# Two MLPs: the norm's factor moved behind the down product, and three small table products moved into the first MLP

## The chip, the cores and the metric

The kernel runs on one core of a Trainium2 chip. The core has a matrix engine (TensorE, PE in the profile, with PEld for its weight loads), a vector engine (VectorE, DVE), an activation engine (ScalarE, ACT), a general engine (GpSimd, POOL), and DMA queues, of which the one of SyncE (SP) carries nearly all loads. The metric is the device time of one execution in microseconds (us), as the median over several runs.

## The reference, cut to what matters

The input is 256 tokens of width 1024 in float32. Two transformer layers follow, each an attention block and then an MLP, and after them a third, different block. Only the MLP, its norm and one bias table matter here:

```python
def rms_norm(x, g):
    y = xf * lax.rsqrt(jnp.mean(xf * xf, axis=-1, keepdims=True) + EPS)
    return y * g

def sq_relu_mlp(h, w_up, w_down):            # D_FF = 4096
    return jnp.square(jax.nn.relu(h @ w_up)) @ w_down

for layer in range(2):
    h = h + attention(...)                   # a different one in each layer
    h = h + sq_relu_mlp(rms_norm(h, mlp_norm[layer]), mlp_w_up[layer], mlp_w_down[layer])
```

The third block has three attention groups of 8 heads each, whose logits get a relative position bias `rel_bias_2[bucket(distance), head]`.

Write r for the factor rsqrt(mean + EPS) of a token. It is positive, so relu(r z) = r relu(z), and the square of that is r*r times relu(z) squared. The factor can therefore be left out ahead of the up product and applied as r*r to the token's row of the down product.

## The kernel before, in words

The residual `hres` stays on the chip as two tiles of 128 tokens, t = 0 and 1, each 128x1024. Every product is made of three single ones: each float32 operand is split into a rounded high part and a remainder (`whi`/`wlo` for weights, `..h`/`..l` for activations), and high x high, high x low and low x high are added up in PSUM. A weight part of 1 MB is loaded by SyncE's queue into one of 3 buffers `raw`, split by ScalarE (L252, high) and VectorE (L255, low) into one of 4 buffers, and used by TensorE.

An MLP, `mlp(i)`, runs like this. The norm (`norm_x`) makes for each t the factor: two squares with a running sum on ScalarE (L175), an add and a scale on VectorE (L177, L156), and the power -1/2 on GpSimd (L158). Then VectorE multiplies the row by factor and gain in two halves (L193), TensorE transposes the 8 blocks (L165) into the two PSUM banks `tr`, and ScalarE and VectorE split the result into `mxh` and `mxl` (L169). The hidden width is done in 8 chunks of 512. Chunk 0 (`up_tok`) is computed token by token, so it can begin with t = 0 alone; chunk 1 and later (`up`, L310 to L313) by feature, with all 256 tokens at once. From chunk 2 on, `step(c - 2)` adds an older chunk to the down product (L361 to L364), which stays in four PSUM banks to the end. `last([6, 7])` finishes the down product, t = 0 first, and adds each half row to the residual (`add_res`, L318).

After the last chunk the first MLP calls `biases_2`, which for three groups loads a 33x512 one-hot table (tile `oh`, L428, from two buffers), multiplies it by 8 columns of the bias table (tile `bt`, L430, in a bank of `tr`), copies the result on ScalarE (`bts`, L432) and stores it from ScalarE's queue to a table `vec_b` in DRAM (L433). The third block reads the tables much later. Then `layer_b` begins: it loads small constants (L441), takes transposes of the unnormed residual (L165) and their split (`bxh`, `bxl`), and multiplies with two narrow matrices, the first with 288 columns (L275 to L278).

The program's order is not the order of each engine. A planner simulates the program, gives each instruction a place in its engine's queue, and prefers, of what is ready, what comes first in the program. Tiles of one name share a few buffers in the order in which the program asks for them. Loads marked `keep_in_program_order` (L441) and instructions inside `behind` are held back on purpose. On the chip each queue then runs strictly in that order.

Of the kernel before, what the change touches and what calls it, by code (L numbers as in the profile page):

```python
# [14 lines left out]
OP = mybir.AluOpType  # L15
# [74 lines left out]
def block_kernel(ctx: ExitStack, tc: tile.TileContext, a, out: bass.AP):  # L90
    nc = tc.nc
    V, A, G, PE = nc.vector, nc.scalar, nc.gpsimd, nc.tensor
# [9 lines left out]
    def nm(s):  # L102
        uid[0] += 1
        return f"{s}_{uid[0]}"

    def t4(s, dt=F32, cols=1024):
        return sp.tile([P, cols], dt, tag="x4", name=nm(s), bufs=N4)

    def t2(s, dt=F32, cols=512):
        return sp.tile([P, cols], dt, tag="x2", name=nm(s), bufs=N2)  # L110

    def tj(s, cols=512):
        return sp.tile([P, cols], F32, tag="sq", name=nm(s), bufs=NSQ)

    def tpt(s):
        return sp.tile([P, 512], F32, tag="pT", name=nm(s), bufs=NPT)

    SMALL = dict(bn=(24, 2), ss=(1, 4), ss2=(2, 4), lr=(1, 2), gk=(64, 1), gkq=(64, 1), gq=(64, 1), kj=(64, 2), kr=(32, 2), krj=(32, 2), kro=(32, 2),
                 l=(16, 6), nx=(16, 6), scq=(4, 8), rr=(16, 8), rv=(16, 4), ce=(8, 6), pre=(16, 2), ssr=(1, 2))

    def sm(s, cols=8):
        w, n = SMALL.get(s, (8, 2))
        return sp.tile([P, w], F32, tag="s_" + s, name=nm(s), bufs=n)
# [7 lines left out]
    def pop(s):  # L131
        return pp.tile([P, 512], F32, tag="po", name=nm(s), bufs=NPO)

    def lgp(s):
        return pp.tile([P, 512], F32, tag="lg", name=nm(s), bufs=NLG)

    def bcast_row(dst, src_1d, n):
        G.dma_start(dst, row(src_1d, n))
# [6 lines left out]
    hres = [cp.tile([P, D], F32, name=f"h{t}") for t in range(2)]  # L145
# [7 lines left out]
    def rsqrt_eps(ss, scale, n, eps=EPS):  # L153

        v = sm("rv", n)
        V.tensor_scalar(v[:, :n], ss, scale, eps, op0=OP.mult, op1=OP.add)  # L156
        r = sm("rr", n)
        G.tensor_tensor(r[:, :n], v[:, :n], mhalf[:, :n], op=OP.pow)  # L158
        return r[:, :n]

    def transposes(src, n, ps=None, w=P):

        ps = trp("tr") if ps is None else ps
        for i in range(n):
            PE.transpose(ps[:w, i * P:(i + 1) * P], src[:, i * w:(i + 1) * w], ident)  # L165
        return ps
# [4 lines left out]
    def rms_stats(h):  # L171
        ss2 = sm("ss2", 2)
        for i in range(2):
            j = tj("sq")
            A.activation(j, h[:, i * 512:(i + 1) * 512], AF.Square, accum_out=ss2[:, i:i + 1])  # L175
        ss = sm("ss", 1)
        V.tensor_tensor(ss[:, :1], ss2[:, 0:1], ss2[:, 1:2], op=OP.add)  # L177
        return rsqrt_eps(ss[:, :1], 1.0 / D, 1)

    def norm_T(h, r, gain, x, t):  # L180

        if r is not None or gain is not None:
            hns = t4("hn")
        for i in range(2):
            c = slice(i * 512, (i + 1) * 512)
            hn = h[:, c] if r is None and gain is None else hns[:, c]
            if gain is None:
                if r is not None:
                    V.tensor_scalar(hn, h[:, c], r, None, op0=OP.mult)
            elif r is None:  # L190
                V.tensor_tensor(hn, h[:, c], gain[:, c], op=OP.mult)
            else:
                V.scalar_tensor_tensor(hn, h[:, c], r, gain[:, c], op0=OP.mult, op1=OP.mult)  # L193
            ps = transposes(hn, 4)
            put(x, i, t, ps.rearrange("p (k n) -> p k n", k=4))

    mark = []
# [9 lines left out]
    def norm_x(x, gain, fold=True):  # L207


        holds, rs = [tuple(mark[1:])], []  # L210
        for t in range(2):
            if fold:
                rs.append(rms_stats(hres[t]))
                norm_T(hres[t], None, gain, x, t)
            else:
                norm_T(hres[t], rms_stats(hres[t]), gain, x, t)
            holds.append(tuple(mark))
        return holds, rs
# [12 lines left out]
    def put(x, i, t, src):  # L231

        mark[:] = split(x[0][i][:, :, t * P:(t + 1) * P], x[1][i][:, :, t * P:(t + 1) * P], src)

    def xs(x, k, t):
        return x[k // 4][:, k % 4, t * P:(t + 1) * P]
# [28 lines left out]
    def wparts(w, KT, c0, n, k0=0, gain=None, by_k=False):  # L265
        return [(g, min(4, KT - g), wsplit(w, k0 + g, min(4, KT - g), c0, n, gain, by_k and g == 0))
                for g in range(0, KT, 4)]
# [47 lines left out]
    def add_res(t, ci, ps, scale=None):  # L315
        h = hres[t][:, ci * 512:(ci + 1) * 512]
        if scale is None:
            V.tensor_tensor(h, ps, h, op=OP.add)  # L318
        else:
            V.scalar_tensor_tensor(h, ps, scale, h, op0=OP.mult, op1=OP.add)  # L320

    def gain_row(src, n=D, s="gain"):
        g = t4(s) if n > 512 else t2(s)
        bcast_row(g[:, :n], src, n)
        return g
# [17 lines left out]
    def down_acc(w, us, nc_):  # L343

        banks = {}

        def bank(ci, t):
            if (ci, t) not in banks:
                banks[ci, t] = pop("dn") if (ci, t) == (1, 1) else lgp("dn")
            return banks[ci, t]  # L350

        def load(c, ci):
            return wparts(w, len_u(us[c]), ci * 512, 512, k0=4 * c)[0]

        def run(c, ci, t, part):
            ps, u = bank(ci, t), us[c]
            kt = len_u(u)
            _, _, (wh, wl) = part
            for k in range(kt):
                s0 = xs(u[0], k, t)  # L360
                PE.matmul(ps, s0, wh[:, k, :], start=(c == 0 and k == 0), stop=False)  # L361
                PE.matmul(ps, s0, wl[:, k, :], start=False, stop=False)  # L362
            for k in range(kt):
                PE.matmul(ps, xs(u[1], k, t), wh[:, k, :], start=False, stop=(c == nc_ - 1 and k == kt - 1))  # L364

        def step(c):
            for ci in range(2):
                part = load(c, ci)
                for t in range(2):
                    run(c, ci, t, part)  # L370

        def last(cs):
            parts = [[load(c, ci) for c in cs] for ci in range(2)]
            for t in range(2):
                for ci in range(2):
                    for c, part in zip(cs, parts[ci]):
                        run(c, ci, t, part)
                    add_res(t, ci, banks[ci, t])
        return step, last

    def mlp(i):
        g = gain_row(a["mlp_norm"][i])
        x = xpair("mx")
        holds, _ = norm_x(x, g, fold=False)
        us = []
        w = a["mlp_w_up"][i]

        def square(ps):
            r = t2("r")
            A.activation(r, ps, AF.Relu)  # L390
            sq = t2("sq")
            A.activation(sq, r, AF.Square)
            return sq

        def up_tok(c):
            u = xpair("u", 4)

            def evac(t, ps):
                tp = transposes(square(ps), 4).rearrange("p (k n) -> p k n", k=4)
                put(u, 0, t, tp)  # L400
            dense_by_tile([(x, 8, w, c * 512, 512, None, evac)], holds=holds[:1])
            us.append(u)

        def up(c):
            u = xpair("u", 4)
            with behind(holds[1] if c == 1 else None):
                parts = wparts(w, 8, c * 512, 512)
            for pr in range(2):
                put_feat(u, pr, square(feat_bank("up", x, parts, pr)))
            us.append(u)  # L410

        step, last = down_acc(a["mlp_w_down"][i], us, 8)
        up_tok(0)
        up(1)
        for c in range(2, 8):
            step(c - 2)
            up(c)
        last([6, 7])
        if i == 0:
            biases_2()  # L420

    def len_u(u):
        return u[0][0].shape[1]

    def bias_rows(which, K, M, c0, vec):

        oh = tpt("oh")
        nc.sync.dma_start(oh[:33, :], a["c_oh"][:, which, :])  # L428
        ps = trp("bt")
        PE.matmul(ps[:M, :], rb[:K, c0:c0 + M], oh[:K, :], start=True, stop=True)  # L430
        sb = tj("bts")
        A.activation(sb[:M, :], ps[:M, :], AF.Copy)  # L432
        nc.scalar.dma_start(vec, sb[:M, :])  # L433

    vec_a = dr.tile([16, 512], F32, name="vec_a")
    vec_b = [dr.tile([8, 512], F32, name=f"vec_b{g}") for g in range(3)]
# [6 lines left out]
    def load_consts():  # L443
# [6 lines left out]
            gcols[nm_] = cp.tile([P, 8], F32, name="gc" + nm_)  # L450
            ldk(gcols[nm_], src.rearrange("(k p) -> p k", p=P))
        return chmask

    def biases_2():
        for g in range(3):
            bias_rows(1 + g, 33, 8, 16 + 8 * g, vec_b[g])

    def quad(tl, Sk):
        return tl[:, :4 * Sk].rearrange("p (h s) -> p h s", h=4)
# [816 lines left out]

    layer_a()
    mlp(0)
    layer_b()
    mlp(1)  # L1280
    block2()
    ffn()
# [27 lines left out]
```

## Time and profile before

| | |
|---|---|
| Runs of the kernel | 1163.79, 1168.25 and 1168.85 us, median 1168.25 |
| The profiled execution's own time | 1167.43 us |
| Its span, first to last instruction | 1165.6 us |
| Mean granted clock of TensorE | 0.99 of full speed |

The span lies 1.83 us under the time of the same execution. In the profile, a row of the timeline shows the start in us from the span's start, the time that it covers, the engine, the line, the operation, the tile written and the tiles read, and how many instructions were merged into it; in brackets stands the idle time of the engine just before, and what ended it. [...]

### The profile page before, as it was taken

The page shows a single profiled execution, that of the slowest core. Times are in us where ns is not written, and L with a number is a line of the kernel's source. Part 1 is how long each engine was busy: PE and PEld are TensorE (multiplying, and loading weights), DVE is VectorE, ACT ScalarE, POOL GpSimd, SP SyncE. Part 2 cuts the span into 40 slices and gives each one's busy share as a digit, 9 for nine tenths or more (in the row PEclk, how much of TensorE's full clock was granted, in tenths as well). Part 3 has the DMA queues.
Part 4 walks back from the last instruction along what each step waited for, and adds up shares of the span by engine and source line. Part 5 has one row for each costly group of instructions (what it writes and reads, how often), then busy time and mean ns, then how long its engine had stood idle before and what let it go on. Part 6 is the DMA issues. An engine that isn't in the chain of part 4 may idle for free.

```text
span 1165.6 us, 17291 instructions
## 1 busy us (share of the span) xinstructions
PE 1130.8 (97%) x6912; PEld 998.9 (86%) x6912; DVE 676.4 (58%) x1190; ACT 613.0 (53%) x1070; POOL 95.9 (8%) x120
## 2 busy tenths in 40 slices
PE   7989999999989999999999999999999999999997
PEld 7767798998778888998989999889888878999996
DVE  6884655445569565445446885665474556544545
ACT  7654554455568455455446564464564435443443
POOL 1310000000048200000000000010000030000000
PEclk9999999999999899999999999999999999999999
DMA  9720646556345126656536644554544434546541
GB/s 287 260 91 5 204 158 216 183 179 179 93 145 178 55 73 217 202 177 202 196 100 236 217 145 145 190 190 137 177 157 145 171 136 162 196 167 216 199 134 65
DMA packets 105383, 191.92 MB, mean 165 GB/s; under 512 B 6616, under 2 KB 22960, under 8 KB 105304
## 3 DMA queue, kind: packets, MB, share of 16 engines
q1 hardware_dynamic: 104072, 187.17, 48.3%
q0 software_dynamic: 1040, 3.54, 1.0%
q8 instruction: 54, 0.88, 0.3%
q14 instruction: 25, 0.20, 0.1%
q10 hardware_dynamic: 192, 0.12, 0.0%
HBM read 189.68 MB, written 1.13 MB: 164 GB/s over the span
## 4 chain that ended last, share of the span: by engine, by line
PE 67%; DVE 1%; issue 1%; POOL 1%; ACT 1%; POOLq 0%; DVEq 0%
PE acc L275 7%; PE acc L276 7%; PE acc L278 7%; PE dn L361 4%; PE dn L362 4%; PE dn L364 4%; PE tr L165 3%; PE up L310 2%; PE up L313 2%; PE up L311 2%; PE po L500 2%; PE qk L311 2%; PE qk L310 2%; PE qk L313 2%; PE fg L311 1%; PE fp L311 1%
## 5 line engine op out<-in xcount | busy, mean ns | idle before, releaser
L255 DVE TENSOR_TENSOR wlo<-raw,whi 128x1024 fp32r<-128x1024 f32 (+3 forms) x340 | 387.0, 1179 | 209.9 <-ACT whi L252 209.2
L252 ACT ACTIVATE whi<-raw 128x1024 fp32r<-128x1024 f32 (+3 forms) x340 | 323.2, 1008 | 209.8 <-PE dn L364 82.8
L310 PE MATMUL up<-mxh,whi 128*128 128x256 f32 x448 | 110.9, 281 | 0.0
L311 PE MATMUL up<-mxl,whi 128*128 128x256 f32 x448 | 110.7, 280 | 0.0
L362 PE MATMUL dn<-wlo,uh 128*128 128x512 f32 x256 | 100.5, 393 | 0.0
L361 PE MATMUL dn<-whi,uh 128*128 128x512 f32 x256 | 100.4, 394 | 0.0
L158 POOL TENSOR_TENSOR rr<-rv,mhalf 128x1 f32<-128x1 f32 (+2 forms) x42 | 42.6, 1017 | 652.5 <-DVE rv L156 630.8
L310 PEld LDWEIGHTS up<-mxh,whi 128*128 128x128 f32 x448 | 84.4, 188 | 0.7
L311 PEld LDWEIGHTS up<-mxl,whi 128*128 128x128 f32 x448 | 84.2, 188 | 0.7
L275 PE MATMUL acc<-whi,cxh 128*128 128x512 f32 (+1 forms) x192 | 74.5, 389 | 0.0
L276 PE MATMUL acc<-wlo,cxh 128*128 128x512 f32 (+1 forms) x192 | 72.4, 378 | 0.0
L313 PE MATMUL up<-mxh,wlo 128*128 128x256 f32 x448 | 70.8, 280 | 0.0
L364 PE MATMUL dn<-whi,ul 128*128 128x512 f32 x256 | 69.6, 394 | 0.0
L313 PEld LDWEIGHTS up<-mxh,wlo 128*128 128x128 f32 x448 | 60.3, 188 | 0.0
L364 PEld LDWEIGHTS dn<-whi,ul 128*128 128x128 f32 x256 | 48.0, 188 | 11.2
L361 PEld LDWEIGHTS dn<-whi,uh 128*128 128x128 f32 x256 | 48.1, 188 | 10.6
L362 PEld LDWEIGHTS dn<-wlo,uh 128*128 128x128 f32 x256 | 48.1, 188 | 10.6
L278 PE MATMUL acc<-whi,cxl 128*128 128x512 f32 (+1 forms) x192 | 50.6, 382 | 0.0
L310 PE MATMUL qk<-cxh,whi 128*128 128x256 f32 x192 | 49.1, 288 | 0.0
L169 DVE TENSOR_TENSOR ul<-sq,uh 128x512 fp32r<-128x512 f32 x28 | 19.4, 692 | 50.6 <-ACT uh L169 50.3
L311 PE MATMUL qk<-cxl,whi 128*128 128x256 f32 x192 | 48.2, 282 | 0.0
L484 ACT ACTIVATE lg<-lg,nx 128x128 f32<-128x128 f32 (+1 forms) x80 | 35.4, 446 | 14.8 <-DVE nx L544 14.6
(413 smaller groups left out, 2443.5 us busy)
## 6 DMA issues: line engine op xcount, KB each, us to landing
raw<-in_w_in SPq DMA_DIRECT2D x38, 1024.0 KB, 5.0
raw<-in_mlp_w_up SPq DMA_DIRECT2D x32, 1024.0 KB
raw<-in_mlp_w_down SPq DMA_DIRECT2D x32, 1024.0 KB, 5.0
raw<-in_w_gate SPq DMA_DIRECT2D x10, 1024.0 KB, 5.2
raw<-in_w_up SPq DMA_DIRECT2D x10, 1024.0 KB, 5.2
raw<-in_w_down SPq DMA_DIRECT2D x10, 1024.0 KB, 4.9
raw<-in_w_in SPq DMA_DIRECT2D x6, 688.0 KB
raw<-in_a_w_in SPq DMA_DIRECT2D x4, 1024.0 KB
```

The costliest lines, as they stand in the source:

```text
L158: G.tensor_tensor(r[:, :n], v[:, :n], mhalf[:, :n], op=OP.pow)
L252: A.activation(hi[:, c], raw[:, c], AF.Copy)
L255: V.tensor_tensor(lo[:, c], raw[:, c], hi[:, c].bitcast(F32), op=OP.subtract)
L275: PE.matmul(o, s0, wh[:, k, :], start=(g + k == 0), stop=False)
L276: PE.matmul(o, s0, wl[:, k, :], start=False, stop=False)
L278: PE.matmul(o, xs(xl, g + k, t), wh[:, k, :], start=False, stop=(g + k == KT - 1))
L310: PE.matmul(o, s0, xh[(g + k) // 4][:, (g + k) % 4, :], start=(g + k == 0), stop=False)
L311: PE.matmul(o, s0, xl[(g + k) // 4][:, (g + k) % 4, :], start=False, stop=False)
L313: PE.matmul(o, wl[:, k, col:col + P], xh[(g + k) // 4][:, (g + k) % 4, :], start=False, stop=(g + k == KT - 1))
L361: PE.matmul(ps, s0, wh[:, k, :], start=(c == 0 and k == 0), stop=False)
L362: PE.matmul(ps, s0, wl[:, k, :], start=False, stop=False)
L364: PE.matmul(ps, xs(u[1], k, t), wh[:, k, :], start=False, stop=(c == nc_ - 1 and k == kt - 1))
```

## The change

The MLP's norm is left without its factor: gain, transposes and split work on the raw residual. The factors are made by a new function `factors`, called after chunk 1: the same statistics, then the factor times itself. `last` passes the two results to `add_res`, which multiplies the PSUM row by it while adding (L320 instead of L318). Both MLPs are changed so. `biases_2` is removed, and its three calls of `bias_rows` are made in the first MLP behind chunks 3, 4 and 5.

```diff
-    SMALL = dict(bn=(24, 2), ss=(1, 4), ...
+    SMALL = dict(r2=(1, 2), bn=(24, 2), ss=(1, 4), ...
...
-        def last(cs):
+        def last(cs, scale=None):
...
-                    add_res(t, ci, banks[ci, t])
+                    add_res(t, ci, banks[ci, t], scale and scale[t])
...
     def mlp(i):
         g = gain_row(a["mlp_norm"][i])
         x = xpair("mx")
-        holds, _ = norm_x(x, g, fold=False)
+        holds = [tuple(mark[1:])]
+        for t in range(2):
+            norm_T(hres[t], None, g, x, t)
+            holds.append(tuple(mark))
+        r2 = []
+
+        def factors():
+            for t in range(2):
+                r = rms_stats(hres[t])
+                q = sm("r2", 1)
+                V.tensor_tensor(q[:, :1], r, r, op=OP.mult)
+                r2.append(q[:, 0:1])
...
         up_tok(0)
         up(1)
+        factors()
         for c in range(2, 8):
             step(c - 2)
             up(c)
-        last([6, 7])
-        if i == 0:
-            biases_2()
+            if i == 0 and 3 <= c <= 5:
+                bias_rows(c - 2, 33, 8, 8 * c - 8, vec_b[c - 3])
+        last([6, 7], r2)
...
-    def biases_2():
-        for g in range(3):
-            bias_rows(1 + g, 33, 8, 16 + 8 * g, vec_b[g])
```

## Rows read from the trace of the kernel before

**Rows 1.** The page's busy times and shares of the span.
```profile
PE 1130.8 (97%) x6912; PEld 998.9 (86%) x6912; DVE 676.4 (58%) x1190; ACT 613.0 (53%) x1070; POOL 95.9 (8%) x120
```

**Rows 2.** A window inside the first MLP (PE, PEld, DVE, ACT, POOL, clock, DMA).
```profile
200.00:285.00 85.00, 85.00 (x557) 77.42 (x556) 39.36 (x37) 43.19 (x52) 1.14 (x2) 1.00 0.55 183
```

**Rows 3.** Timeline of TensorE, start of the first MLP.
```profile
125.91 1.09 PE L278 MATMUL acc<-whi,mxl 128*128 128x512 f32 x4
129.21 1.75 PE L165 MATMUL tr<-ident,hn 128*128 128x128 f32 x8 [2.21 <-DVE hn L193]
...
133.67 0.28 PE L310 MATMUL up<-mxh,whi 128*128 128x256 f32 x1
```

**Rows 4.** Timeline of VectorE, the same stretch.
```profile
120.38 1.28 DVE L318 TENSOR_TENSOR h<-acc,h 128x512 f32<-128x512 f32 x2
...
128.31 1.42 DVE L193 SCALAR_TENSOR_TENSOR hn<-h,rr,gain 128x512 f32<-128x512 f32 x2 [0.45 <-POOL rr L158]
```

**Rows 5.** Windows around idle stretches of TensorE (columns as in rows 2).
```profile
129.20:133.00 3.80, 3.79 (x14) 2.99 (x15) 1.91 (x3) 1.19 (x2) 0.00 (x0) 0.55 0.86 285
...
310.20:314.00 3.80, 3.80 (x18) 3.37 (x18) 2.86 (x16) 3.35 (x8) 0.00 (x0) 0.55 0.12 25
...
306.20:308.20 2.00, 1.93 (x5) 0.27 (x4) 0.69 (x1) 0.59 (x1) 0.00 (x0) 1.00 0.03 9
...
321.30:322.90 1.60, 0.00 (x0) 0.00 (x0) 0.70 (x3) 0.67 (x2) 0.87 (x2) 1.00 0.07 27
322.90:326.00 3.10, 3.06 (x23) 3.06 (x24) 1.53 (x4) 1.37 (x3) 0.00 (x0) 1.00 0.01 3
```

**Rows 6.** Timeline of TensorE, end of the first MLP, start of layer_b.
```profile
305.23 1.09 PE L364 MATMUL dn<-whi,ul 128*128 128x512 f32 x4
306.25 1.88 PE L430 MATMUL bt<-oh,rb 33*8 33x512 f32 x4
309.32 1.02 PE L430 MATMUL bt<-oh,rb 33*8 33x512 f32 x2 [1.19 <-DMA oh<-in_c_oh]
310.26 1.86 PE L165 MATMUL tr<-ident,h 128*128 128x128 f32 x8
311.89 0.61 PE L275 MATMUL acc<-whi,bxh 128*128 128x288 f32 x1
...
313.96 0.60 PE L165 MATMUL tr<-ident,h 128*128 128x128 f32 x4
```

**Rows 7.** Timeline of SyncE's queue, the same stretch.
```profile
307.30 0.32 SPq L428 DMA_DIRECT2D oh<-in_c_oh  x1
307.67 0.38 SPq L441 DMA_DIRECT2D rp<-in_c_rope  x1
```

**Rows 8.** Timeline of TensorE, start of the second MLP.
```profile
436.67 1.04 PE L165 MATMUL tr<-ident,hn 128*128 128x128 f32 x8
438.01 0.50 PE L275 MATMUL acc<-whi,mxh 128*128 128x512 f32 x1 [0.30 <-ACT mxh L169]
```

**Rows 9.** Single lines: instructions, and ns as minimum, median and maximum.
```profile
L320 DVE SCALAR_TENSOR_TENSOR h<-acc,h x4: 681/688/692, 957.6 to 970.4; 128x512 f32<-128x512 f32 x4
...
L193 DVE SCALAR_TENSOR_TENSOR hn<-h,rr,gain x16: 744/746/752, 102.5 to 973.8; 128x512 f32<-128x512 f32 x16
...
L175 ACT ACTIVATE sq<-h x28: 613/630/637, 3.5 to 1159.8; 128x512 f32<-128x512 f32 x28
```

**Rows 10.** Timelines of ScalarE, VectorE and TensorE in mid MLP.
```profile
211.11 0.60 ACT L390 ACTIVATE r<-up 128x512 f32<-128x512 f32 x1 [3.63 <-PE up L313]
...
214.89 3.90 ACT L252 ACTIVATE whi<-raw 128x1024 fp32r<-128x1024 f32 x4 [1.85 <-PE up L311]
...
215.99 4.63 DVE L255 TENSOR_TENSOR wlo<-raw,whi 128x1024 fp32r<-128x1024 f32 x4 [2.22 <-ACT whi L252]
...
216.56 0.39 PE L361 MATMUL dn<-whi,uh 128*128 128x512 f32 x1
...
227.75 0.28 PE L310 MATMUL up<-mxh,whi 128*128 128x256 f32 x1
```

More of the change, by code (lines that the diff above doesn't have):

```diff
@@ L116, in tpt @@
         return sp.tile([P, 512], F32, tag="pT", name=nm(s), bufs=NPT)
-    SMALL = dict(bn=(24, 2), ss=(1, 4), ss2=(2, 4), lr=(1, 2), gk=(64, 1), gkq=(64, 1), gq=(64, 1), kj=(64, 2), kr=(32, 2), krj=(32, 2), kro=(32, 2),
+    SMALL = dict(r2=(1, 2), bn=(24, 2), ss=(1, 4), ss2=(2, 4), lr=(1, 2), gk=(64, 1), gkq=(64, 1), gq=(64, 1), kj=(64, 2), kr=(32, 2), krj=(32, 2), kro=(32, 2),
                  l=(16, 6), nx=(16, 6), scq=(4, 8), rr=(16, 8), rv=(16, 4), ce=(8, 6), pre=(16, 2), ssr=(1, 2))
```

## The prediction

> **What bounds the kernel now.** I read the page first: TensorE is busy for 97% of the span [rows 1], so I take the time to be TensorE's queue plus its gaps, and any other engine's work to cost nothing while TensorE is fed. The windows inside the MLPs bear this out: 85.00 us busy out of 85.00, at full clock, with VectorE and ScalarE at half load [rows 2]. A change here can pay only where TensorE stands still, and in what its clock does after a standstill. So I listed the waits of TensorE's queue and went to the timelines of the three places that the diff touches.
>
> At the start of the first MLP the last four products of token tile 0 begin at 125.91, and then TensorE waits 2.21 us for VectorE's `hn`, the normed row of tile 1 [rows 3]. On VectorE the residual was complete at 121.66 (120.38 + 1.28), but `hn` began only at 128.31, behind GpSimd's factor [rows 4]: 6.7 us went by for the statistics. [...]
>
> At the end of the first MLP the last down products begin at 305.23. Then come two bias products, a wait of 1.19 us for the third one-hot table, the third product, and only then the transposes for layer_b; the first product of layer_b begins at 311.89 [rows 6]. The queue of SyncE shows why the table was late: two buffers hold the first two, so the third load was issued at 307.30, after the first product [rows 7]. Again the clock is 0.55, from 310.2 to 314.0 [rows 5]. The second MLP starts better: its second transposes wait for nothing, and 0.30 us is lost before the next product [rows 8].
>
> **The norm, first MLP.** Removed ahead of the transposes are the statistics of both tiles; the multiplication by factor and gain becomes one by gain. It costs 0.746 us per half row now [rows 9], and with one operand fewer I take it as no dearer. With the residual whole at 121.66 the two halves can be ready near 123.2 (121.66 + 2 x 0.75), more than two microseconds before the last products of tile 0 begin, so the transposes can go between them without a wait. What would stay of the stretch: products of 512 columns come every 0.233 us (48 of them between 216.56 and 227.75 [rows 10]), so tile 0's stream ends at 125.91 + 4 x 0.233 = 126.84. Until 133.67 TensorE did 8 transposes and 8 such products. At full clock these are at most 1.04 [rows 8] and 8 x 0.233 = 1.87, together 2.9, where 6.83 passed. Gain 3.9 us. The lower bound is that `hn` keeps its place in VectorE's queue and only its 0.45 us of waiting for GpSimd goes [rows 4]: 0.5. I take 3.9, since the residual is there so long before.
>
> **The norm, second MLP.** The 0.30 us before 438.01 goes the same way [rows 8]: 0.3, between 0 and 0.6.
>
> **The factors.** They come back as four squares on ScalarE, 0.63 us each [rows 9], 2.5 us per MLP, and a few operations on single columns. They stand behind chunk 1, and nothing reads them until the last additions, behind the last chunk. What hides them is the reserve of the weight splits: the four casts that begin at 214.89 and VectorE's halves of them are done by 220.62 (215.99 + 4.63), and TensorE goes on to the next chunk only at 227.75 [rows 10], so about 7 us of lead remain. Cost 0, or 2.5 if that lead were gone.
>
> **The scaled addition.** The trace has no `add_res` in the MLP with a column of factors. The nearest is L320, which does the same with a constant: 0.688 us for the half row out of PSUM; with a column and two SBUF operands it is 0.746 [rows 9]. So 0 to 0.06 us each, of which one per MLP is exposed: 0. [...]
>
> **The bias products, where they were.** From 306.16 (305.23 + 4 x 0.233) to 313.96 TensorE did the six bias instructions, 8 transposes and 8 products of 288 columns [rows 6]. Without the bias the transposes of tile 0 come first: its residual has long been added. In the second MLP it is 1.34 us from the start of such transposes to the first product [rows 8]. The 8 products took 2.07 at mostly half clock, so some 1.04 at full. That is 2.4 instead of 7.8: gain 5.4. What could be late next is the split `bxl` on VectorE, were it queued behind operations on the constants, whose loads stood behind the third table in SyncE's queue [rows 7]; that queue is now free of it, so I expect them earlier. If they bind all the same, I put the gain at half, 2.7.
>
> **The bias products, where they go.** Six instructions at 0.43 us (four take 0.86 longer than two, 1.88 against 1.02 [rows 6]) are 2.6 us in a stretch without gaps: paid in full. ScalarE gets the three copies and their three DMA issues, under the same 7 us of lead; behind them stand casts, for which TensorE would wait last. SyncE gets the third load earlier, behind the first product; the other two were already loaded long ahead.
>
> **Sum.** 3.9 + 0.3 + 5.4 - 2.6 = 7.0 us of 1167.43, the profiled execution's own time (span 1165.6 and 1.83 around it): 1160.4. The median of the runs is 0.8 higher, from which it would be 1161.2; I give 1160.8.
>
> **The rivals.** A: the next wait takes the place of the bias gap in layer_b, and the move gains 2.7 - 2.6 = nothing: gain 4.2, or 1163.6. For it: layer_b waits for short chains elsewhere, such as 1.6 us idle at 321.3 [rows 5]. Against: tile 0's residual is ready, and nothing else stands in its way that I see.
>
> B: the planner keeps tile 1's `hn` behind the splits of chunk 1, so the change doesn't do there what it says. The first term falls from 3.9 to 0.5: 1164.2. For it: VectorE stood idle for only 0.45 us ahead of `hn` [rows 4], so it had other work between. Against: the planner prefers what comes first in the program, and `hn` does.
>
> C: the clock falls at the light bias products in mid MLP. A fall as at 129.2 costs 0.45 x 3.8 = 1.7 us [rows 5]; three cost 5.1: 1165.9. For it: at 310.2 the clock was down although the idle wait before was only 1.2 us, after products of 33 rows and 8 columns; an idle 1.6 us at 321.3 left it at 1.00 [rows 5]. Against: 1.9 us of those very products ran at 1.00 [rows 5], and each pair now lasts 0.86 us between dense work. [...]
>
> D, slower: a bias copy stands in ScalarE's queue ahead of the casts, and waits there for a product that TensorE has placed behind a half chunk of 11.2 us (216.56 to 227.75 [rows 10]). It decides from a wait of 7 us on. At three places this is 3 x (11.2 - 7) = 12.6, and a fall of the clock each, 5.1: 1178.5. For it: both queues are strict. Against: ScalarE's wait for TensorE there is 3.63 us [rows 10], and the planner would have to be wrong by a multiple of that.
>
> **How the numbers follow.** Forecast 0.60, A 0.15, B 0.12, C 0.06, D 0.07. One half per cent, 5.8 us, is about what a measurement of this kernel can tell from no change; the bound is 1162.4. The forecast lies under it, D above 1174.1, the others between: faster 0.60, same 0.33, slower 0.07. The range begins at 1157.0: the sum from the profiled execution (1160.4) with 0.3 more in the second MLP, the 1.6 us wait of layer_b gone, since ScalarE is freer there, and one fall of the clock fewer (1.7). It ends at 1167.0, where A and B meet (2.8 and 3.4 above the forecast); C lies inside.
>
> **What would show it.** After the change TensorE has no wait for `hn` at the first MLP's start and a clock of 1.00 there; transposes of `h` follow directly on the last L364 at the end, and the first product of layer_b comes 1.3 us later; the span from the first MLP's start to there is shorter by 3.9 - 2.6 up to the last L364, and by 5.4 more after it. Six L430 instructions stand in mid MLP, at 0.43 us, with PEclk 1.00. The additions are L320 at about 0.7 us. I am wrong if windows in mid MLP are no longer full, or if what was gained is lost again in layer_b's attention, whose clock I have left as it was.

## The result, and the profile after

The kernel after takes 1160.54 us as the median of 5 runs (1155.89 to 1161.48), the kernel before 1168.25 beside it (5 runs, 1163.79 to 1169.15). The ratio is 0.9934 with a 95% interval of 0.9917 to 0.9951: faster by 7.7 us. That is more than the half per cent (5.8 us) that the prediction set, though the near end of the interval, 5.7 us, does not clear it. Forecast were 1160.8 us, and a chance of 0.60 for faster by that much. The profiled execution after took 1161.48 us with a span of 1159.7; the one before took 1167.43.

The page shows TensorE as busy as before [rows 1]:

```profile
PE 1128.4 (97%) x6912; PEld 996.8 (86%) x6912; DVE 675.7 (58%) x1194; ACT 612.0 (53%) x1070; POOL 95.1 (8%) x120
```

The timeline of TensorE after, from the first norm of the first MLP to the second MLP:

```profile
103.71 0.66 PE L165 MATMUL tr<-ident,o 128*128 128x128 f32 x4 [1.27 <-DVE o L695]
...
128.11 1.10 PE L278 MATMUL acc<-whi,mxl 128*128 128x512 f32 x4
129.05 1.03 PE L165 MATMUL tr<-ident,hn 128*128 128x128 f32 x8
130.39 0.50 PE L275 MATMUL acc<-whi,mxh 128*128 128x512 f32 x1 [0.30 <-ACT mxh L169]
...
132.35 0.28 PE L310 MATMUL up<-mxh,whi 128*128 128x256 f32 x1
...
192.93 1.02 PE L443 MATMUL bt<-oh,rb 33*8 33x512 f32 x2
193.88 0.50 PE L361 MATMUL dn<-whi,uh 128*128 128x512 f32 x1
...
307.36 1.10 PE L364 MATMUL dn<-whi,ul 128*128 128x512 f32 x4
308.29 1.04 PE L165 MATMUL tr<-ident,h 128*128 128x128 f32 x8
309.58 0.40 PE L275 MATMUL acc<-whi,bxh 128*128 128x288 f32 x1 [0.25 <-ACT bxh L169]
...
310.74 0.60 PE L165 MATMUL tr<-ident,h 128*128 128x128 f32 x4
...
318.58 0.44 PE L165 MATMUL tr<-ident,lc 128*128 128x128 f32 x2 [0.50 <-DVE lc L768]
...
356.99 0.64 PE L165 MATMUL tr<-ident,k 128*96 128x128 f32 x4 [1.74 <-POOL k L831]
...
381.29 0.77 PE L165 MATMUL tr<-ident,p 128*128 128x128 f32 x2 [1.66 <-ACT p L493]
...
412.59 0.38 PE L165 MATMUL tr<-ident,oB 128*128 128x128 f32 x2
...
424.67 0.60 PE L165 MATMUL tr<-ident,hn 128*128 128x128 f32 x4
425.02 0.48 PE L275 MATMUL acc<-whi,mxh 128*128 128x512 f32 x1
...
432.02 0.50 PE L275 MATMUL acc<-whi,mxh 128*128 128x512 f32 x1 [0.30 <-ACT mxh L169]
...
433.99 0.28 PE L310 MATMUL up<-mxh,whi 128*128 128x256 f32 x1
```

Four rows of the kernel before, for the places that the rows ahead of the prediction do not show:

```profile
101.52 0.66 PE L165 MATMUL tr<-ident,o 128*128 128x128 f32 x4 [0.79 <-DVE o L686]
...
322.94 0.44 PE L165 MATMUL tr<-ident,lc 128*128 128x128 f32 x2 [1.65 <-DVE lc L759]
...
418.07 0.38 PE L165 MATMUL tr<-ident,oB 128*128 128x128 f32 x2
...
439.98 0.28 PE L310 MATMUL up<-mxh,whi 128*128 128x256 f32 x1
```

Read against [rows 3], the wait of 2.21 us for tile 1's `hn` is gone: the transposes follow tile 0's last products at 129.05. From those products to the first L310 it is now 4.24 us (128.11 to 132.35), where it was 7.76. Read against [rows 6], the transposes of `h` follow the last L364, and from that L364 to the second transposes it is 3.38 us (307.36 to 310.74), where it was 8.73. One wait is longer: at 103.71 TensorE waits 1.27 us for `o`, and it was 0.79 before (101.52).

VectorE's timeline shows why, for better and for worse:

```profile
102.36 0.69 DVE L191 TENSOR_TENSOR hn<-h,gain 128x512 f32<-128x512 f32 x1
102.97 0.68 DVE L695 TENSOR_TENSOR o<-po,rl 128x512 f32<-128x512 f32 x1
...
122.58 1.28 DVE L318 TENSOR_TENSOR h<-acc,h 128x512 f32<-128x512 f32 x2
...
124.44 1.28 DVE L191 TENSOR_TENSOR hn<-h,gain 128x512 f32<-128x512 f32 x2
```

The residual of tile 1 is whole at 123.86, and `hn` begins at 124.44 without waiting for a factor. For tile 0 the same readiness puts an `hn` ahead of the attention's `o`, for which TensorE stands still.

Windows of the kernel after (columns as in rows 2, the clock being that granted to TensorE as a share of full speed): the start of the first MLP, mid MLP with two of the bias places, the start of layer_b, and two stretches of layer_b's attention.

```profile
129.00:132.80 3.80, 3.50 (x22) 2.85 (x21) 2.84 (x7) 2.09 (x4) 0.56 (x1) 1.00 1.00 316
...
200.00:285.00 85.00, 85.00 (x547) 75.69 (x546) 37.63 (x35) 41.62 (x52) 0.00 (x0) 1.00 0.53 177
...
307.30:311.00 3.70, 3.45 (x24) 2.94 (x24) 2.01 (x5) 2.07 (x5) 0.40 (x1) 1.00 0.35 121
...
340.00:370.00 30.00, 25.97 (x147) 22.41 (x146) 25.20 (x60) 23.92 (x59) 26.40 (x37) 0.94 0.53 176
370.00:400.00 30.00, 27.96 (x177) 25.61 (x175) 18.00 (x50) 15.22 (x43) 10.92 (x15) 0.89 0.26 88
```

The clock is 1.00 at both places where it was 0.55 [rows 5], and mid MLP is full. But in layer_b's attention the granted clock falls to 0.50 in both executions: for 10.2 us in all after (358 to 363 and 382 to 390 us), and for 13.6 us before (361 to 366 and 385 to 396). These times are added up from windows of 1 us: a window at 0.50 counts whole, one at 0.75 half. The execution after has one more fall, of 3.4 us at 75 to 79 us, ahead of everything that was changed. What a fall costs shows at the first MLP's start in the kernel before, on TensorE's timeline:

```profile
124.07 0.39 PE L275 MATMUL acc<-whi,mxh 128*128 128x512 f32 x1
...
125.69 0.39 PE L276 MATMUL acc<-wlo,mxh 128*128 128x512 f32 x1
...
131.24 0.63 PE L276 MATMUL acc<-wlo,mxh 128*128 128x512 f32 x1
...
132.94 0.42 PE L276 MATMUL acc<-wlo,mxh 128*128 128x512 f32 x1
```

The first two rows begin and end 8 products in a row at 1.00, the last two 5 products while the clock was down: one came every 0.23 us there (1.62 / 7) and every 0.43 us here (1.70 / 4). So, as an estimate from these, each microsecond of a fall costs up to 0.46, and the 10.2 us up to 4.7, as much as a term of the sum. The prediction left these stretches as they were; the experiments had to ask whether that is safe.

### The profile page after: what moved, and what is told of

Its sections match the earlier page's. It is cut to its first block, busy times and chain, and to the rows that moved or that the text cites. A ratio compares the mean times of both kernels' runs of the same rounds, so it can differ in the third digit from the quotient of the medians.

```text
span 1159.7 us, 17292 instructions
## 1 busy us (share of the span) xinstructions
PE 1128.4 (97%) x6912; PEld 996.8 (86%) x6912; DVE 675.7 (58%) x1194; ACT 612.0 (53%) x1070; POOL 95.1 (8%) x120
## 4 chain that ended last, share of the span: by engine, by line
PE 91%; DVE 4%; ACT 2%; issue 1%; POOL 1%; DMA 0%; SPq 0%; POOLq 0%; DVEq 0%
PE acc L275 10%; PE acc L276 9%; PE acc L278 9%; PE dn L361 7%; PE dn L362 7%; PE dn L364 7%; PE up L310 5%; PE up L313 5%; PE up L311 5%; PE tr L165 4%; PE po L509 3%; PE qk L311 2%; PE qk L310 2%; PE lg L485 2%; PE qk L313 2%; PE fg L311 1%
## 5 line engine op out<-in xcount | busy, mean ns | idle before, releaser
L310 PE MATMUL up<-mxh,whi 128*128 128x256 f32 x448 | 111.2, 281 | 0.0
L361 PE MATMUL dn<-whi,uh 128*128 128x512 f32 x256 | 100.7, 395 | 0.0
L310 PEld LDWEIGHTS up<-mxh,whi 128*128 128x128 f32 x448 | 84.4, 188 | 0.7
L364 PE MATMUL dn<-whi,ul 128*128 128x512 f32 x256 | 69.6, 394 | 0.0
L361 PEld LDWEIGHTS dn<-whi,uh 128*128 128x128 f32 x256 | 48.1, 188 | 13.2 <-ACT whi L252 2.6
L364 PEld LDWEIGHTS dn<-whi,ul 128*128 128x128 f32 x256 | 48.1, 188 | 11.2
L310 PE MATMUL qk<-cxh,whi 128*128 128x256 f32 x192 | 49.1, 288 | 0.0
L175 ACT ACTIVATE sq<-h 128x512 f32<-128x512 f32 x28 | 17.5, 627 | 49.4 <-DVE h L318 23.0
```

The source lines that it names most:

```text
L310: PE.matmul(o, s0, xh[(g + k) // 4][:, (g + k) % 4, :], start=(g + k == 0), stop=False)
```

## The experiments

Each kernel is timed beside the kernel before, whose median was 1167.72 us (35 runs) beside the first four, 1167.48 (20) beside the next four and 1168.14 (11) beside the last four; its runs spread there over 8.8, 6.2 and 1.6 us.

**The same kernel again.** The kernel after, unchanged.

> The changed kernel once more, nothing edited. In its first trace the clock fell between 74 and 80 us, long before the first changed instruction, which the kernel before did not show there (0.62 against 1.00 from 76 to 80), and everything up to the first MLP came about 1.7 us late. Theory: that fall is chance of one execution, and here the clock stays at 1.00 there; the time is 6.5 to 8 us under the kernel before. Rival: it comes with the changed order of the queues, and shows again.

Measured: 1160.62 us (12 runs, 1155.89 to 1162.35), ratio 0.9939 [0.9921, 0.9958]. Its profiled execution took only 1156.29 us, and the windows show why:

```profile
340.00:370.00 30.00, 25.17 (x151) 21.62 (x150) 26.22 (x66) 24.05 (x61) 24.59 (x34) 1.00 0.56 182
370.00:400.00 30.00, 27.84 (x205) 25.12 (x204) 19.43 (x51) 17.23 (x52) 10.92 (x15) 1.00 0.23 81
```

The same program, with the clock at 1.00 throughout layer_b; the fall at 75 to 79 us did not come again either. Its waits there are the ones of the execution above, on the timeline of TensorE:

```profile
355.36 0.64 PE L165 MATMUL tr<-ident,k 128*96 128x128 f32 x4 [1.76 <-POOL k L831]
...
379.21 0.77 PE L165 MATMUL tr<-ident,p 128*128 128x128 f32 x2 [1.66 <-ACT p L493]
```

After 1.76 and 1.66 us of standing still the clock stayed up here; after 1.74 and 1.66 it fell there. Over the 12 runs time and mean granted clock go together: three of 1155.89 to 1156.29 us at 0.998, nine of 1159.55 to 1162.35 at 0.991 to 0.994. The kernel before does the same: 1160.99 at 0.997, 1169.82 at 0.989. So a run's time holds falls that the program does not fix.

**Each part alone.** First the norm, then the bias products:

```diff
+    def biases_2():                 # norm alone: called after last() in the first MLP, as before
...
+            if i == 0 and 3 <= c <= 5:      # bias alone: the norm as before
+                bias_rows(c - 2, 33, 8, 8 * c - 8, vec_b[c - 3])
```

> Only the norm's half of the change in both MLPs; the bias products stay at the end of the first MLP. Theory of the prediction: 3.9 + 0.3 = 4.2 us under the kernel before; no wait for the normed row at the first MLP's start, and the wait for the third table at its end is still there. Rival: the MLP's start was covered anyway, so that what this half gains is given back at the end, and nearly all of the 7 us came from the bias products: under 1.5 us.

> Only the bias half: the three products in the middle of the first MLP, the norm as before. Theory of the prediction: 5.4 - 2.6 = 2.8 us under the kernel before. Rival, from the first trace of the changed kernel, in which a chunk with bias products lasts 23.6 us against 22.4: the middle costs 3.4 rather than 2.6, and one wait of layer_b shrinks as well by 1.1: 3.0 to 3.2. Second rival: this half is worth nothing, 0.

Measured: norm alone 1164.23 us (12 runs, 1159.28 to 1167.33), ratio 0.9979 [0.9960, 0.9997]; bias alone 1159.82 (12 runs, 1157.70 to 1166.20), ratio 0.9950 [0.9930, 0.9970]. By the medians they give 3.5 and 7.9 us: 11.4 together, where both at once give 7.1. By the ratios they give 2.5 and 5.8, each to within some 2 us, so that the gap to 7.1 is hardly clear of the noise. By the medians of these two kernels the bias would be worth twice its term and the norm would hurt beside it. Against that reading: nine of the 12 bias runs had a clock of 0.996 to 0.999 and three (1164.83 to 1166.20 us) one of 0.990 or 0.991, while eleven of the 12 norm runs had 0.988 to 0.993. The two kernels drew different falls. Why the one drew them so much more seldom than the other stays open; timed plainly, bias alone (0.9950) and both parts (0.9939) are not told apart.

**The table earlier.** The kernel before with the third one-hot table in another buffer, so that its load waits for nothing; the products stay at the MLP's end.

```diff
-        oh = tpt("oh")
+        oh = tlq("oh") if which == 3 else tpt("oh")
```

> The kernel before, with one edit: the third one-hot table is loaded into a buffer of another kind, so that all three are there long before the end of the first MLP and the constants of layer_b are not held up behind the third. The products stay at the end, between the down product and layer_b. Theory: the price of the old place was the late table and the fall of the clock after it, not the place; six products of 0.43 us are paid in either place. Then this alone gains about what moving them gains, 2.5 to 3.5 us. Rival: the place itself costs, since the products also hold the two banks that the transposes need: only the wait of 1.2 us goes, 1.0 to 1.5 us.

Measured: 1166.82 us (12 runs, 1164.78 to 1168.27), ratio 1.0002 [0.9986, 1.0018]. The wait for the table is gone and layer_b's first product comes 1.3 us earlier in the profiled executions, but the whole does not move measurably. The interval allows a gain of at most 1.6 us, so the theory's 2.5 to 3.5 is refuted: the late table and its wait were not most of the price. The rival's 1.0 to 1.5 us lies inside the interval. The fall behind the products is still there, from 310 to 314 us.

**The clock held up in layer_b.** The kernels after and before, each with 29 products that nobody reads, placed where TensorE waits in layer_b's attention. They write a bank that the transposes behind them overwrite; all else is as it was.

```diff
+FILL = {("k", 1, 0): 13, ("k", 1, 1): 3, ("p", 2, 0, 0): 13}
-    def transposes(src, n, ps=None, w=P):
+    def transposes(src, n, ps=None, w=P, fill=0, early=None):
         ps = trp("tr") if ps is None else ps
+        for _ in range(fill):
+            PE.transpose(ps[:w, :P], ident[:, :w], ident) if early is None else PE.transpose(ps[:64, :P], early, ident)
```

> The kernel after, with 29 products that nobody reads added in layer_b's attention: 13 and 3 ahead of the transposes of k, and 13 ahead of the transposes of p, where TensorE waited 1.74, 0.51 and 1.66 us in the profiled execution and the granted clock was down soon afterwards (358 to 363 and 382 to 390 us, together 10.2 us low, worth 5.1 us). Theory (standing still there is what lets the clock fall, in some executions and not in others): no fall between 340 and 400 us, the waits shorter by 1 us and more but the work behind them no later, 1155.5 to 1157 us, and hardly any run above 1158.5. Rival 1 (the falls do not come from these waits): the clock is down at the same places as before, 1160 to 1162 us. Rival 2 (the added products stand in the way): the products cost 29 times about 0.11 us, 3.2 us, in spite of a clock that stays up: 1158.5 to 1160.

> The kernel before, with the same 29 unread products at the same places of layer_b's attention. Theory: the falls at 361 to 366 and 385 to 396 us (13.6 us low, worth 6.8) are gone, those at the first MLP's start and end (3.4 us low each) stay: 1161 to 1163 us, and the kernel after with the same products is faster than it by 5.5 to 7, the prediction's sum. Rival 1 (falls do not come from these waits): 1167 to 1168.5. Rival 2 (the added products cost 3 us): 1164 to 1166.

Measured: after 1159.55 us (5 runs, 1158.95 to 1159.76), before 1166.61 (11 runs, 1165.28 to 1167.02). Windows and timeline of the kernel after with these products:

```profile
60.00:70.00 10.00, 8.06 (x39) 5.74 (x38) 9.21 (x51) 7.20 (x33) 3.76 (x3) 0.83 0.53 184
340.00:370.00 30.00, 26.55 (x163) 22.65 (x162) 25.77 (x60) 23.29 (x57) 24.96 (x34) 1.00 0.56 179
370.00:400.00 30.00, 27.40 (x197) 24.42 (x197) 18.15 (x51) 16.57 (x49) 11.16 (x15) 1.00 0.26 85
```

```profile
353.78 1.58 PE L166 MATMUL tr<-ident,k 128*64 128x128 f32 x13
355.70 0.64 PE L168 MATMUL tr<-ident,k 128*96 128x128 f32 x4 [0.34 <-POOL k L834]
...
382.31 1.64 PE L166 MATMUL tr<-ident 128*128 128x128 f32 x13 [0.82 <-DVE pT L505]
```

The falls in layer_b are gone in both profiled executions. Over all the runs of this document, seven of the eight profiled executions without unread products have a fall between 340 and 400 us, and none of the six with them. The spread of the runs is 0.8 us after (5 runs; without the products 6.5 in 12) and 1.7 before (11 runs; without them 6.2 in the 20 timed beside). By itself a small spread shows little: beside the last four kernels the kernel before spread over 1.6 us too, with falls in every run by its clock (0.989 to 0.991). That is in keeping with the theory's cause; its times were not met. Expected were 1155.5 to 1157 and 1161 to 1163 us. Two things are in the way: a fall of 3.4 us that remains at 63 to 67 us, and the 13 products at 382.31, which came after a wait of 0.82 for their bank instead of in it, and lie on the path (rival 2, in part). In layer_b the exchange is poor: from its first product to the first product of its output projection (`boh`) it is 80.04 us in the kernel after with its two falls, 79.43 with the unread products, and 76.54 in the execution that had neither. What the pair is good for is the difference: 1166.61 - 1159.55 = 7.06 us. The unread products are transposes, and no fall followed them: from 340 to 400 us the clock is 1.00 in both.

**Each part alone, with the clock held up.** The same two edits as above on the kernel before, each with the 29 products.

> The kernel before with the norm's part of the change alone (both MLPs), and with the 29 unread products in layer_b's attention, which took the falls of the clock there away and brought the kernel before to 1166.61 and the kernel after to 1159.55 us, 7.06 apart. Theory (the two parts of the change add up, and it was the falls in layer_b that made norm alone, 3.5 us, and bias alone, 7.9 us, give more than the 7.1 of both): the norm is worth its 3.5 us at the first MLP's start, less 0.45 at the wait for o, and 0.9 at the second MLP's start, 4.0 us: 1162.6. Rival (norm alone is really worth 3.5 of 11.4 and the parts get in each other's way): 1163.1 or more here, and bias alone below 1160.

> The kernel before with the bias products' part of the change alone, and with the same 29 unread products in layer_b. Theory (the parts add up): 5.35 at the start of layer_b and 1.1 at the narrow product's wait there, less 3.45 in the first MLP, 3.0 us: 1163.6, and together with the norm's part the 7.06 of both within 0.7. Rival (bias alone is worth 7.9 us, as measured without the added products): 1158.7.

Measured: norm 1162.65 us (5 runs, 1161.43 to 1163.68), bias 1163.54 (5 runs, 1162.40 to 1164.28). Against 1166.61 that is 3.96 and 3.07 us, together 7.03, where both at once give 7.06. The theory said 4.0, 3.0 and 7.06. The rival is refuted where it is clear of the noise: it wanted 1158.7 of the bias, whose fastest run took 1162.40. These two kernels were timed apart from the 1166.61, and the kernel before was 0.66 us higher beside them; by the ratios to it the parts are 4.0 and 3.3 and both at once 7.2. With five runs each, spread over some 2 us, the sum may be off by about one us, so an agreement to 0.03 is luck.

The profiled executions of the four kernels say it without medians. Three starts on TensorE's timeline, and the stretches between them:

| with the 29 products | tile 0's last products | last product `dn<-whi,ul` | first `boh` | first stretch | second stretch |
|---|---|---|---|---|---|
| before | 126.44 | 306.16 | 394.68 | 179.72 | 88.52 |
| norm alone | 126.76 | 302.58 | 390.80 | 175.82 | 88.22 |
| bias alone | 127.29 | 310.25 | 391.91 | 182.96 | 81.66 |
| both | 126.82 | 306.07 | 387.72 | 179.25 | 81.65 |

In the first stretch the norm takes away 3.90 us without the bias and 3.71 with it, and the bias adds 3.24 and 3.43. In the second the bias takes away 6.86 and 6.57, and the norm 0.30 and 0.01. So the parts add up to within 0.3 us once the falls in layer_b are out of the way. By windows of 1 us each part takes its own old fall along: with the norm alone the clock is still down at 308 to 312 us, with the bias alone at 131 to 135.

**The bias products three times.** The kernel after, with each of the three products in mid MLP computed three times.

```diff
-        PE.matmul(ps[:M, :], rb[:K, c0:c0 + M], oh[:K, :], start=True, stop=True)
+        for _ in range(3 if which else 1):
+            PE.matmul(ps[:M, :], rb[:K, c0:c0 + M], oh[:K, :], start=True, stop=True)
```

> The kernel after, with each of the three products of the second bias table computed three times in the middle of the first MLP (the same result written again). Theory (paid in full, clock untouched): each of the 6 added products takes 0.86 us, 5.2 us, on top of about 1.15 us that each place costs now; the chunks there last about 25.3 us instead of 23.6, the granted clock stays at 1.00, 1165.5 to 1166.5 us. Rival C (light products among dense ones let the clock fall): with 2.6 us of them together the clock falls at the three places, 1.7 us each, 1169 to 1171. Rival (they lie beside other work): below 1162.

Measured: 1165.37 us (10 runs, 1162.89 to 1168.15), 4.8 above the kernel after. Timeline of TensorE, then windows:

```profile
192.86 0.51 PE L361 MATMUL dn<-whi,uh 128*128 128x512 f32 x1
...
215.49 2.74 PE L444 MATMUL bt<-oh,rb 33*8 33x512 f32 x6
218.16 0.51 PE L361 MATMUL dn<-whi,uh 128*128 128x512 f32 x1
...
245.05 0.51 PE L361 MATMUL dn<-whi,uh 128*128 128x512 f32 x1
```

```profile
215.00:219.00 4.00, 4.00 (x15) 1.50 (x15) 4.00 (x4) 3.84 (x6) 0.00 (x0) 1.00 0.12 10
219.00:223.00 4.00, 4.00 (x12) 3.13 (x11) 1.15 (x2) 1.01 (x2) 0.00 (x0) 0.58 1.04 396
```

From one L361 to the next it is 25.30 us (192.86 to 218.16), as expected, where the kernel after takes 23.57 (193.88 to 217.45): 1.73 for two products more, 0.86 each, paid in full. The next stretch is 26.89, since the clock fell behind the second place, from 219 to 223. So a fall as rival C of the prediction has it was seen here, although TensorE never stood still there. It was seen once, at one place of three, with 2.7 us of light products together; behind the 1.0 us of the kernel after no profiled execution shows it.

**The bias products in layer_b's waits.** The kernel after, with the three products not in the first MLP but in layer_b's attention, ahead of three head groups.

```diff
-            if i == 0 and 3 <= c <= 5:
-                bias_rows(c - 2, 33, 8, 8 * c - 8, vec_b[c - 3])
...
-PLAN_B = "k0 q0 k2 20 q1 k1 30 21 *2 q2 31 ...
+PLAN_B = "k0 q0 k2 20 q1 k1 b0 30 21 *2 q2 b1 31 ...
```

> The kernel after, with the three bias products not in the first MLP but in layer_b's attention, ahead of the transposes of three head groups, where TensorE waits for GpSimd. Theory (they are paid only where TensorE is full): the 3.45 us that they cost in the first MLP come back and little is lost in layer_b: 1157 to 1158 us, faster than the kernel after, if the clock in layer_b falls as often as there. Rival 1 (attention is bound by ScalarE, VectorE and GpSimd in turn, and three copies of 0.7 us in ScalarE's queue delay it): 1159.5 to 1161. Rival 2 (the products keep TensorE going in the waits and the clock up): 1153 to 1155.

Measured: 1161.57 us (5 runs, 1159.01 to 1162.42), not below the kernel after. From the first L310 to the last L364 it is 171.58 us (131.35 to 302.93) instead of 175.01, so the MLP gave its 3.43 back. But attention lost more: from layer_b's first product to the first L310 of the second MLP it is 129.76 us (305.15 to 434.91), where it was 124.41 (309.58 to 433.99). Timeline of TensorE:

```profile
355.45 0.50 PE L275 MATMUL acc<-whi,cT 128*128 128x512 f32 x1 [2.24 <-ACT qj L811]
...
376.09 1.02 PE L441 MATMUL bt<-oh,rb 33*8 33x512 f32 x2 [2.01 <-DMA oh<-in_c_oh]
```

One wait of 2.24 us stands behind ScalarE, and the third product waits 2.01 us for its table again, as in [rows 6]. The clock was down for 13.6 us there. Rival 1 was nearest; the copies that it puts at 0.7 us take 0.57 to 0.59 in the kernel after (L445).

**The two old falls filled.** The kernel before with the 29 products and 26 more, 17 behind tile 0's transposes at the first MLP's start and 9 ahead of the third bias product.

```diff
-                norm_T(hres[t], rms_stats(hres[t]), gain, x, t)
+                norm_T(hres[t], rms_stats(hres[t]), gain, x, t, fill)       # 17, first half of tile 1, first MLP
...
         ps = trp("bt")
+        for _ in range(fill):                                               # 9, third table
+            PE.transpose(ps[:, :P], ident, ident)
```

> The kernel before, with the 29 unread products in layer_b and 26 more: 17 at the start of the first MLP, behind the transposes of token tile 0 and so within the 2.2 us that TensorE would stand still later, and 9 ahead of the third bias product, which waited 1.19 us for its table. All waits stay, only TensorE works in them. Theory (of the change's 7.06 us, 3.4 are the two falls of the clock at 131 to 136 and 312 to 316 us): both falls go, 1163.0 to 1163.5 us. Rival 1 (the time is in the waits, and a fall more or less is made up for by the next wait): 1166.6. Rival 2 (the 17 products come where TensorE had none to wait for): 1165 and more, with the clock at 1.00.

Measured: 1164.86 us (7 runs, 1163.84 to 1167.13). Timeline of TensorE, then windows:

```profile
121.48 2.02 PE L166 MATMUL tr<-ident 128*128 128x128 f32 x17
...
307.51 1.20 PE L434 MATMUL bt<-ident 128*128 128x128 f32 x9
308.75 1.02 PE L435 MATMUL bt<-oh,rb 33*8 33x512 f32 x2
```

```profile
129.00:137.00 8.00, 7.16 (x37) 5.71 (x37) 4.58 (x6) 5.03 (x7) 0.00 (x0) 1.00 0.53 179
305.00:315.00 10.00, 9.83 (x55) 6.11 (x54) 5.12 (x20) 6.36 (x13) 0.00 (x0) 1.00 0.19 51
```

Both falls are gone, and the kernel gains 1.75 us on the kernel with the 29 by the medians, timed apart, where 3.4 were expected; the two profiled executions differ by 1.5 at the MLP's start and 1.3 behind its end. The added products cost nothing at either place: tile 1's transposes come 8.76 us behind tile 0's, where it was 8.86, and the third bias product 3.05 behind the first, where it was 3.03. So a fall of 3.4 us at these places costs somewhat less than its half, and of the change's 7.06 us at least 4.3 are waits and products, the rest clock. Between 1.75 and 2.8 for the clock's share the runs don't decide.

**The cheapest version.** The kernel after with 20 of the 29 products (4 instead of 13 ahead of `p`), and in the first attention one product of q and k made four times more, where TensorE waited 1.77 us for a mask.

```diff
+FILL = {("k", 1, 0): 13, ("k", 1, 1): 3, ("p", 2, 0, 0): 4}
...
+        for _ in range(rep):                  # 4, second product of the first token tile
+            PE.matmul(lg, q, k, start=True, stop=True)
         PE.matmul(lg, q, k, start=True, stop=mask is None)
```

> The kernel after, with 20 of the 29 unread products in layer_b (4 instead of 13 ahead of the transposes of p, where all 13 were on the path) and the product of q and k at the start of the first attention made four times more, where TensorE waited 1.77 us for a mask and the clock was down afterwards (63 to 67 us) in the kernel with all 29. Theory: that fall goes too (1.7 us) and 9 products fewer give 1.0 us: 1156.5 to 1157.3, all runs within 1 us, faster than both kernels. Rival 1 (4 products are too few to keep the clock up at the wait for p): it falls again at 380 to 390 us in some runs, 1158.5 to 1160. Rival 2 (the four products delay the first attention): 1158 to 1159 with the clock at 1.00.

Measured: 1158.36 us (5 runs, 1157.80 to 1159.54), ratio 0.9919 [0.9905, 0.9932]. The window that had the fall before:

```profile
60.00:70.00 10.00, 8.92 (x48) 6.28 (x48) 9.89 (x52) 7.15 (x35) 3.62 (x3) 1.00 0.53 182
```

By windows of 1 us no fall is left but at the kernel's very end. The median is 2.2 us below the kernel after, which was timed apart, and 9.8 below the kernel before. It missed its 1156.5 to 1157.3 by 1.1 us: layer_b takes 1.9 us longer to the output product than in the execution of the unchanged kernel that had no falls (78.44 against 76.54), and why more than the four products (0.66) is lost there stays open. The ratio's interval overlaps that of the kernel after (0.9921 to 0.9958), so that it beats it is likely and not shown. What is shown is the steadier clock: 0.998 or 0.999 in all five runs, where the kernel after had that in three of 12.

## Why the prediction was right

**The norm, first MLP: right, 0.4 too high.** Forecast 3.9, measured 7.76 - 4.24 = 3.52 us. VectorE's `hn` came where it was expected (rival B did not happen), but behind the transposes 0.30 us of waiting for the split stays, which the sum had at nothing.

**The norm, second MLP: the size right in order, the place wrong.** The 0.30 us [rows 8] that should go stayed (432.02). Instead tile 0's part gained: half of its transposes came 9 us earlier, and a wait of 0.25 us for the first split is gone (424.67, 425.02). The transposes that moved are paid in their new place, so what is left is 0.51 us (the expectation of the norm with the clock held up had counted 0.9): from the last transposes of `oB` to the first L310 it is 21.40 us (412.59 to 433.99), where it was 21.91 (418.07 to 439.98). In all 14 profiled executions this stretch is 21.39 to 21.41 with the new norm and 21.90 to 21.93 with the old.

**Missing from the sum: the wait for `o`.** An `hn` that is ready earlier stands ahead of other work on VectorE. It costs 1.27 - 0.79 = 0.48 us at 103.71. The three add up to 3.55, where the forecast was 4.2. The runs with the clock held up gave 3.96. There the old fall at the MLP's start came a little later and the norm took away 3.90 instead of 3.52 in the first stretch of the table; with that the three make 3.93.

**Factors and scaled addition: right.** With the norm alone, and so with the factors but without the bias products in the MLP, it is 171.57 us from the first L310 to the last L364 (130.48 to 302.05), where it was 171.56 before: the factors cost nothing. The additions are L320 at 0.75 us, by lines of the kernel after:

```profile
L320 DVE SCALAR_TENSOR_TENSOR h<-dn,r,h 128x512 f32<-128x512 f32 x8 | 6.0, 750 | 17.7 <-PE dn L364 17.7
```

Rival D did not happen: mid MLP is full at 1.00.

**The bias products, old place: right.** Forecast 5.4, measured 8.73 - 3.38 = 5.35. On top, the next wait in layer_b, for `lc`, fell from 1.65 to 0.50 us (322.94 before, 318.58 after). The prediction had it only at the range's low end, and rival A had expected the reverse.

**The bias products, new place: mis-sized.** Forecast 2.6, measured 3.45: from the first L310 to the last L364 it is 175.01 us (132.35 to 307.36), where it was 171.56. With the bias alone it is 174.97 (134.61 to 309.58), so this is the bias products' own. The term counted 0.86 us for each product and nothing around it. The repeated products cost 0.86 each, so what was missing is 0.2 to 0.3 at each of three places; where it comes from was not shown. In all: 5.35 + 1.15 - 3.45 = 3.05, measured alone 3.07 by the medians and 3.1 to 3.6 by the table's rows, forecast 2.8.

**The sum: right, in part by luck.** Forecast 7.0; 3.55 + 3.05 = 6.6 by the rows above; 7.06 by the medians with layer_b's clock held up; 7.7 and 7.1 by the plain medians. Of the four terms only the bias products' old place was met to 0.1 us. The norm's first term and the new place were 0.4 and 0.85 too favourable, and 0.48 at `o` was missing; 0.2 more at the second MLP and 1.15 at `lc`, which the sum did not have, nearly make up for them. One of the prediction's signs came out otherwise for that reason: up to the last L364 the MLP was to be 1.3 us shorter, and it is 0.07 (179.25 from tile 0's last products, where it was 179.32). The lower end of the range, by its own terms, is 1156.8 and not 1157.0; nothing hangs on it.

What the working left out is layer_b's clock. The single parts, timed plainly, missed by 0.5 to 5 us through it; that the plain medians fit as well is luck too: away from the two places of the change, and from the last microseconds, in which TensorE has no work, the clock was down for 13.6 us in the profiled execution before and for 13.6 in the one after (by windows of 1 us).

## What to carry to other kernels

A fall of the clock in the trace of one execution was not a constant of the program here (0.89 from 370 to 400 us in one, 1.00 in the next): profile the same kernel twice, and set the mean granted clock of every run beside its time, before a difference of one half per cent is put down to an edit. Where edits measured one by one don't add up, quiet the clock with unread products in the waits of both kernels and measure them again; compare the pair, since the added products cost time themselves (here 2.9 us). Better still, read the time between two fixed instructions around each edit: with the clock at 1.00 it repeated to 0.03 us here, while the medians leave about one. And a small product moved into a full stretch was paid in full here, 0.86 us each with 0.2 to 0.3 us more at each place, so it pays to move it only if the old place cost a wait as well.

## What the runs showed of the hardware

The same waits, 1.74 and 1.76 us at one instruction, were followed by a fall of the granted clock to 0.50 in one execution and by none in another of the same program. By windows of 1 us the falls took from 3.4 to 10.2 us, and one of 3.4 at the old places cost 1.3 to 1.5 us by the rows. Once a fall came without any standstill, behind 2.7 us of products of 33 rows and 8 columns in a busy TensorE (219 to 223 us); at two other such places none came. In the kernels in which unread products filled the waits of layer_b's attention, the clock was 1.00 from 340 to 400 us in each of the six profiled executions; of the eight without them, seven had a fall there.
